# The g projections of layer 1 by seven block products, and the sums of weight blocks on GpSimd

## The chip, the core and the metric

The kernel runs on one core of a Trainium2 chip. The core has five engines with an instruction queue each: TensorE (PE, with its weight loads shown apart as PEld), VectorE (DVE), ScalarE (ACT), GpSimd (POOL) and SyncE (SP, which issues DMAs here). The metric is the device time of one execution in microseconds; lower is better.

## The reference

One step of a two-layer recurrent decoder for 512 prompt tokens and 8 sample tokens (520 columns, computed together). The change is in layer 1, the HGRN2 layer with 16 heads of 128:

```python
def layer_c(h, p, s_c, lb, norm_w, w_in, c_norm_w, w_out, ple_w, ple_g):
    u = rmsnorm(h, norm_w) @ w_in                       # 1024 -> 4 x 2048
    q, fx, v, gate = jnp.split(u, [HK_C, 2 * HK_C, 2 * HK_C + D_C], axis=-1)
    g = jnp.logaddexp(jnp.log(lb), jnp.log1p(-lb) + jax.nn.log_sigmoid(fx))
    k = (1.0 - lb) * jax.nn.sigmoid(-fx)
    o, new_c = hgrn2_scan(q * DK_C ** -0.5, k, v, g, s_c)   # per head, chunkwise
    o = o * lax.rsqrt(jnp.mean(o * o, axis=-1, keepdims=True) + EPS)
    o = o.reshape(Bsz, L, D_C) * c_norm_w * jax.nn.silu(gate)
    h = h + o @ w_out
    ...
```

In the kernel, f, v, q and g are the four projections fx, v, q and gate; g is only needed at the end of a head, as silu.

## The kernel before

All projections are done in halves of precision: each fp32 matrix is split into a rounded fp32r part and the rest, and a product is the sum of three matmuls, high by high, high by low, low by high. Activations are split once (`xh1`, `xl1`, each 8 slices of 128 rows by 520 columns). Weights are split as they come: a group of 256 columns (1 MB, tile `wraw`, two buffers) is loaded by SyncE, ScalarE writes the high part (`whir`, a CAST), VectorE the low part (`wlor`, wraw minus whir). In layer 1 these two are rings that hold four halves of 128x512.

Layer 1 goes through eight pairs of heads. A pair `pr` has four groups of weights in the order f, v, q, g; each yields 256 rows by 520 columns, that is 128 rows for each of its two heads. An ordinary projection (`project_both`) takes 8 slices x 3 x 2 column halves = 48 matmuls of 128x260 for each head. In pairs 1 to 7, f and v go another way, by `strassen`: the group is taken as a 2x2 block matrix (two halves of the 8 slices, two heads), the activations as 2x2 as well (two halves of the slices, two column halves), and seven block products of 4 x 3 = 12 matmuls stand in for eight. For that, sums of weight blocks are needed, four for each group, each 128x512, done in place or into the tiles named f1s, v1s and so on; sums of the activation blocks (`uh`, `ul`) are made once. The products come out in PSUM (tiles `sm` and `sg`) and are summed on VectorE into the SBUF tiles `l1a` (f) and `l1b` (v and g). Between the products TensorE does the heads' own work (A, kt, kv, o, ot, vt), and every second round the output projection (tile `o`), whose results are added to `h`.

q and g of every pair, and all of pair 0, are ordinary projections. `evac_g` takes a finished g tile from PSUM: ScalarE writes tanh(g/2) to `l1b`, VectorE makes (tanh + 1) times the PSUM tile.

GpSimd does little in layer 1: the small powers by which the heads normalize (`at__`, 128x4 and 16x1).

No order is written by hand. The code records operations, and `Plan.order` sets them out, engine by engine, from a cost for each operation, with engines as independent of one another; each engine then runs its list in order. Operations that TensorE's main products need are given urgency; some copies and scalings may go to ScalarE or VectorE, as the plan finds room. Nearly every instruction therefore has the line of the recording helper, L520, and tiles tell them apart. The change thus moves the order all through layer 1.

Of the kernel before, what the change touches and what calls it, by code (L numbers as in the profile page):

```python
# [15 lines left out]
AF = mybir.ActivationFunctionType  # L16
# [5 lines left out]
MUL, ADD, SUB, MAX, MIN = ALU.mult, ALU.add, ALU.subtract, ALU.max, ALU.min  # L22
# [3 lines left out]
N = T + NS  # L26
HN = N // 2
# [182 lines left out]
class Plan:  # L210
# [53 lines left out]
    @contextmanager  # L264
    def block(self, main=False):

        self.open = Op(self, self.pos + self.shift, 0)
        self.open.forms["pe"] = [[], 0.0, None]
        self.open.main = main
        self.open.ins, self.open.outs = [], []  # L270
        yield
        op, self.open = self.open, None
        op.forms["pe"][1] /= 2400.0
        self.add(op, op.ins, op.outs)
# [266 lines left out]
def hybrid_decode_step_kernel(ctx: ExitStack, tc: tile.TileContext, I, O, mode="both"):  # L541
# [19 lines left out]
    act, dve, pool, pe, sp = (Engine(plans, k) for k in ("act", "dve", "pool", "pe", "sp"))  # L561
    side, block = (lambda *a, **k: plans[-1].side(*a, **k)), (lambda *a: plans[-1].block(*a))

    def new(pool_, shape, tag, name, bufs=1, dt=F32):
        return plans[-1].tile(pool_, shape, dt, tag, name, bufs, {"psm": PSUM, "psa": PSUM, "drp": DRAM}.get(pool_, SBUF))
# [4 lines left out]
    def mmps(name):  # L570
        return new("psm", [128, 2, 512], "mm", name, 2)

    def grab(name):

        return new("psa", [128, 512], "ax", name)

    def halves(ap):
        return ap.rearrange("p (a b) -> p a b", a=2)

    def ps520(ps):  # L580
        return ps[:, :, :HN]
# [4 lines left out]
    def tt(out, a, b, op, eng=dve):  # L586
        eng.tensor_tensor(out=out, in0=a, in1=b, op=op)

    def stt(out, a, s, b, op0, op1):
        dve.scalar_tensor_tensor(out=out, in0=a, scalar=s, in1=b, op0=op0, op1=op1)  # L590
# [7 lines left out]
    def fn(out, in_, func, **kw):  # L598
        act.activation(out, in_, func, **kw)

    def copy(out, in_):

        plans[-1].record(("act", "copy", (out, in_), {}), ("dve", "tensor_copy", (out, in_), {}))
# [6 lines left out]
    def slot(tag, name, shape=None, dt=F32):  # L610
        return new("lay", shape or [128, KT, N], tag, name, dt=dt)
# [17 lines left out]
    def load_group(g):  # L629
        ap, k0, kk, c, w = groups[g]  # L630
        r = new("wp", [128, 2048], "raw", f"wraw{g}", 2)
        v = r[:, :kk * w].rearrange("p (k c) -> p k c", k=kk)
        with side(*((plans[-1].shift, 0.0, True) if plans[-1].pinned else (-LOAD_AHEAD,))):
            sp.dma_start(out=v, in_=ap[k0 * 128:(k0 + kk) * 128, c:c + w].rearrange("(k p) c -> p k c", p=128))
        raw_of[g] = v
# [9 lines left out]
    def split_half(v):  # L645

        hv, lv = (r.rearrange("p (k c) -> p k c", k=4) for r in ring_space(1))
        with side(-SPLIT_AHEAD):
            act.copy(hv, v)
            tt(lv, v, hv.bitcast(F32), SUB)  # L650
        return hv, lv
# [300 lines left out]
    mx, e0, e1, sm, lb, omlb, lb60, oml60, lbf, omf, cneg, cq, ch, fb = (lbt[:, i] for i in range(14))  # L952
# [658 lines left out]
    def layer1_fast():  # L1611
        NO = 4
        A = None
        B = slot("acy", "l1b", [128, 4160])
# [42 lines left out]
        H = [{} for _ in range(NH)]  # L1657

        def start_f(hd):
            nonlocal A  # L1660
            d, p = H[hd], hd % 2
            if A is None:
                A = slot("w", "l1a", [128, 4160])
            d["t"] = A[:, p * N:(p + 1) * N]
            d["b"] = A[:, 1040 + p * N:1040 + (p + 1) * N]

            d["s4"] = s4s[hd // 2 % 2][:, :, p]
            return d["t"]

        def done_f(hd, tanh=True):  # L1670
            d = H[hd]
            if tanh:
                fn(d["t"], d["t"], AF.Tanh, scale=0.5)
            t = d["t"][:, T:]
            ts(d["s4"][:, 0], t, -1.0, ADD, cneg[:, hd:hd + 1], MUL)
            ts(d["s4"][:, 1], t, ch[:, hd:hd + 1], MUL, fb[:, hd:hd + 1], ADD)
# [6 lines left out]
        def done_v(hd):  # L1683
            d, v = H[hd], B[:, hd % 2 * N:(hd % 2 + 1) * N]
            copy(d["s4"][:, 3], v[:, T:])
            with side(V_LATE):
# [3 lines left out]
                        pe.transpose(pv[:, c * 128:(c + 1) * 128], v[:, c * 128:(c + 1) * 128], ident)  # L1690
                copy(d["vt"], pv)

        def evac_f(hd):
            def f(ps):
                fn(halves(start_f(hd)), ps520(ps), AF.Tanh, scale=0.5)
                done_f(hd, False)
            return f
# [7 lines left out]
        def strassen(pr, names):  # L1705

            pss, n = [], 0

            def product(u, x):
                nonlocal n  # L1710

                i = n % 6
                if i % 3 == 2:
                    out = grab(f"sg{pr}_{n}")[:, :HN]
                else:
                    if i < 2:
                        pss[i:] = [mmps(f"sm{pr}_{n}")]
                    out = pss[i % 3][:, i // 3, :HN]
                n += 1
                hw, lw = u  # L1720
                for k in range(4):
                    with block(True):
                        for i, (w, b) in enumerate(((hw, x[0]), (hw, x[1]), (lw, x[0]))):
                            pe.matmul(out, lhsT=w[:, k], rhs=b[:, k], start=(k == 0 and i == 0), stop=(k == 3 and i == 2))
                    plans[-1].pos += 0.334
                return out

            def steps(nm):
                e, e1 = 2 * pr, 2 * pr + 1
                start, done = (start_f, done_f) if nm == "f" else (start_v, done_v)  # L1730
                o0, o1 = start(e), start(e1)
                l0, r0, l1, r1 = o0[:, :HN], o0[:, HN:], o1[:, :HN], o1[:, HN:]
                g = units[sec[f"{nm}{pr}"]][0]
                if g not in raw_of:
                    load_group(g)
                v = raw_of[g]
                a11, a12, a21, a22 = v[:, :4, :128], v[:, 4:, :128], v[:, :4, 128:], v[:, 4:, 128:]
                s2, s3 = (new("cst", [128, N], "sgt", f"{nm}{pr}s{i}", 2)[:, :512].rearrange("p (k c) -> p k c", k=4)
                          for i in range(2))
                w = split_half(a11)  # L1740
                with side(-SPLIT_AHEAD):
                    tt(s3, a11, a21, ADD)
                    tt(a21, a21, a22, ADD)
                    tt(s2, a21, a11, ADD)
                p1 = product(w, x11)
                copy(l0, p1)
                p6 = product(split_half(s2), u2)
                tt(r0, l0, p6, ADD)
                p7 = product(split_half(s3), t3)
                tt(l1, p7, r0, SUB)  # L1750
                w = split_half(a12)
                with side(-SPLIT_AHEAD):
                    tt(a12, a12, s2, ADD)
                p2 = product(w, x21)
                tt(l0, l0, p2, ADD)
                p5 = product(split_half(a21), u1)
                tt(r1, l1, p5, SUB)
                tt(r0, r0, p5, ADD)
                p3 = product(split_half(a12), x22)
                tt(r0, r0, p3, ADD)  # L1760
                done(e)
                p4 = product(split_half(a22), u4)
                tt(l1, l1, p4, ADD)
                done(e1)

            for nm in names:
                steps(nm)
# [9 lines left out]

        def evac_g(hd):
            def f(ps):
                sg = H[hd]["sg"] = B[:, 1040 + (hd % 2) * N:1040 + (hd % 2 + 1) * N]  # L1780
                fn(halves(sg), ps520(ps), AF.Tanh, scale=0.5)
                stt(halves(sg), halves(sg), 1.0, ps520(ps), ADD, MUL)
            return f
# [136 lines left out]
        def pair(pr, names):  # L1920
            a = 2 * pr
            if pr:
                strassen(pr, names[:2])
                with side(DECAY_LATE):
                    decay(a)
                names = names[2:]
            for nm in names:
                ev = {"f": evac_f, "v": evac_v, "q": evac_q, "g": evac_g}[nm]
                tiles = [(sec[f"{nm}{pr}"] + i, 0, ev(a + i), f"{nm}{a + i}") for i in range(2)]
                if pr == 0 and nm == "f":  # L1930
                    project_both(tiles, XN, K8)
                else:
                    for t in tiles:
                        project_both([t], XN, K8)
                if nm == "f":
                    with side(DECAY_LATE):
                        decay(a)
                if nm == "q" and pr in (2, 4, 6):
                    chunk(f"o{pr}", 2 * pr - 4, 2 if pr == 6 else 4, add_to_h)
# [325 lines left out]
```

## Time and profile before

| | |
|---|---|
| median of 3 runs | 1056.26 us (1055.57 to 1057.36) |
| profiled execution | 1052.58 us, span of its instructions 1050.9 us |
| granted TensorE clock | 0.994 |
| layer 1's heads in the trace | about 447 to 952 us |

Durations below come from the profiled execution, which is 3.7 us shorter than the median. On the page, busy is time in which an engine works; matmuls are pipelined, so their durations overlap. In names, `l1a<-l1a,sm` is the tile written and those read.

### The profile page before, as it was taken

What the parts mean: (1) busy time and instruction counts of PE and PEld (TensorE: products, weight loads), DVE (VectorE), ACT (ScalarE), POOL (GpSimd) and SP (SyncE); (2) the same over time, 40 slices, a digit from 0 to 9 for tenths busy, and PEclk for the clock granted to TensorE, in tenths of its full rate; (3) what the DMA queues carried; (4) which work ended last, traced back from release to release, by engine and by line L of the source; (5) the groups of instructions that cost most, each with busy time, mean ns of one, the idle gap of its engine ahead of it and who ended that gap; (6) DMA issues with size and microseconds to landing.
All of it is one profiled execution on the core that took longest, in us unless ns stands there. A gap on an engine that the chain in (4) does not pass through costs nothing.

```text
span 1050.9 us, 21517 instructions
## 1 busy us (share of the span) xinstructions
PE 1023.1 (97%) x8427; PEld 1000.0 (95%) x8427; DVE 832.6 (79%) x1705; ACT 630.8 (60%) x1482; POOL 139.4 (13%) x241
## 2 busy tenths in 40 slices
PE   9989899999999999999999999999999999999995
PEld 8989899899999999999999999999999999999995
DVE  6789788998996656697989759698598979868853
ACT  6588876654673222365676726678268685764553
POOL 4635854100000000001000000001000000100000
PEclk9999999999999999999999999999999999999998
DMA  9712254336586223553353433433434443553311
GB/s 285 246 30 92 81 166 141 122 110 191 188 257 213 89 98 117 153 203 90 98 149 109 142 91 108 139 100 113 122 90 139 124 116 111 137 180 121 121 41 45
DMA packets 129957, 138.45 MB, mean 132 GB/s; under 512 B 13704, under 2 KB 111128, under 8 KB 129832
## 3 DMA queue, kind: packets, MB, share of 16 engines
q1 hardware_dynamic: 129464, 136.64, 42.6%
q8 instruction: 68, 1.11, 0.4%
q10 hardware_dynamic: 160, 0.30, 0.1%
q14 instruction: 41, 0.34, 0.1%
q0 software_dynamic: 224, 0.06, 0.0%
HBM read 111.71 MB, written 25.44 MB: 131 GB/s over the span
## 4 chain that ended last, share of the span: by engine, by line
PE 73%; DVE 10%; DMA 6%; ACT 4%; POOL 3%; issue 2%; SPq 0%; POOLq 0%; ACTq 0%; DVEq 0%
PE o L520 10%; PE sm L520 9%; PE q L520 9%; PE pg L520 9%; PE g L520 8%; PE ob L520 4%; PE sg L520 4%; PE xbc L520 2%; PE ax L520 2%; DVE wlo L520 2%; PE oa L520 2%; PE pl L520 2%; PE z L520 1%; DMA smp<-in_state_b_ssm_dram 1%; POOL csm L520 1%
## 5 line engine op out<-in xcount | busy, mean ns | idle before, releaser
L520 ACT CAST whir<-wraw 128x512 fp32r<-128x512 f32 (+1 forms) x121 | 96.3, 798 | 83.9 <-PE o L520 40.6
L520 DVE TENSOR_TENSOR wlor<-wraw,whir 128x512 fp32r<-128x512 f32 (+1 forms) x121 | 109.6, 910 | 12.5 <-ACT whir L520 12.1
L520 ACT CAST whi<-wraw 128x1024 fp32r<-128x1024 f32 (+1 forms) x56 | 57.8, 1032 | 48.6 <-PE ob L520 34.5
L520 POOL TENSOR_TENSOR at__1738<-at__1738,nhalf 128x4 f32<-128x4 f32 (+1 forms) x24 | 22.6, 942 | 461.5 <-DVE at__1738 L520 455.5
L520 DVE TENSOR_TENSOR wlo<-wraw,whi 128x1024 fp32r<-128x1024 f32 (+1 forms) x64 | 77.3, 1208 | 8.0 <-ACT whi L520 7.4
L520 PE MATMUL o<-ohl,whir 128*128 128x260 f32 x512 | 83.0, 284 | 0.0
L520 PEld LDWEIGHTS o<-ohl,whir 128*128 128x128 f32 x512 | 70.0, 188 | 0.9 <-issue 0.6
L520 PE MATMUL g<-xh,whir 128*128 128x260 f32 x256 | 54.6, 294 | 1.1 <-DVE l1a L520 1.1
L520 PE MATMUL q<-xh,whir 128*128 128x260 f32 x256 | 53.2, 289 | 0.0
L520 PE MATMUL q<-xh,wlor 128*128 128x260 f32 x256 | 51.5, 283 | 0.0
L520 PE MATMUL q<-xl,whir 128*128 128x260 f32 x256 | 51.4, 282 | 0.0
L520 PE MATMUL g<-xl,whir 128*128 128x260 f32 x256 | 51.4, 282 | 0.0
L520 PE MATMUL g<-xh,wlor 128*128 128x260 f32 x256 | 51.4, 282 | 0.0
L520 PE MATMUL o<-ohl,wlor 128*128 128x260 f32 x256 | 51.4, 282 | 0.0
L520 DVE TENSOR_TENSOR h<-h,o 128x520 f32<-128x520 f32 x40 | 27.8, 694 | 26.2 <-PE o L520 25.9
L515 ACT ACT_TABLE_LOAD x36 | 46.2, 1283 | 0.6
L520 PE MATMUL sm<-uh,whir 128*128 128x260 f32 x140 | 40.4, 289 | 1.8 <-DVE l1a L520 1.6
L520 PE MATMUL sm<-xh,whir 128*128 128x260 f32 x140 | 41.4, 296 | 0.0
L520 PEld LDWEIGHTS g<-xh,whir 128*128 128x128 f32 x256 | 39.2, 189 | 2.2 <-DVE l1a L520 1.3
L520 PE MATMUL sm<-xh,wlor 128*128 128x260 f32 x140 | 39.6, 283 | 0.3 <-DVE wlor L520 0.3
L520 PE MATMUL xbc<-xnh,whi 128*128 128x260 f32 x192 | 39.7, 289 | 0.0
L520 PE MATMUL sm<-xl,whir 128*128 128x260 f32 x140 | 39.6, 283 | 0.0
(609 smaller groups left out, 3594.2 us busy)
## 6 DMA issues: line engine op xcount, KB each, us to landing
wraw<-in_c_w_in_dram SPq DMA_DIRECT2D x32, 1024.0 KB
wraw<-in_ab_w_in_dram SPq DMA_DIRECT2D x15, 1024.0 KB
wraw<-in_ab_w_out_dram SPq DMA_DIRECT2D x8, 1024.0 KB
wraw<-in_ple_gate_dram SPq DMA_DIRECT2D x8, 1024.0 KB
wraw<-in_c_w_out_dram SPq DMA_DIRECT2D x8, 1024.0 KB
pl<-pl_d SPq DMA_DIRECT2D x2, 2080.0 KB
smp<-in_state_b_ssm_dram SPq DMA_DIRECT2D x8, 512.0 KB
acy<-acsT_d SPq DMA_DIRECT2D x8, 512.0 KB
```

The source lines that it names most:

```text
L515: self.engines["act"].preload_act_table_set(SETS[table])
L520: getattr(f, name)(*a, **k)
```

## The change

The groups g of pairs 1 to 7 go through `strassen` too, each in a call of its own, with `start_g` and `done_g` at its ends. `done_g` takes the tanh from SBUF into the pair's f buffer `t` and multiplies in SBUF. The sums of weight blocks of all three (f, v and g) are recorded for GpSimd instead of VectorE.

```diff
+        def start_g(hd):
+            sg = H[hd]["sg"] = B[:, 1040 + (hd % 2) * N:1040 + (hd % 2 + 1) * N]
+            return sg
+
+        def done_g(hd):
+            sg, t = H[hd]["sg"], H[hd]["t"]
+            fn(t, sg, AF.Tanh, scale=0.5)
+            stt(sg, t, 1.0, sg, ADD, MUL)
...
                 with side(-SPLIT_AHEAD):
-                    tt(s3, a11, a21, ADD)
-                    tt(a21, a21, a22, ADD)
-                    tt(s2, a21, a11, ADD)
+                    tt(s3, a11, a21, ADD, pool)
+                    tt(a21, a21, a22, ADD, pool)
+                    tt(s2, a21, a11, ADD, pool)
...
                 with side(-SPLIT_AHEAD):
-                    tt(a12, a12, s2, ADD)
+                    tt(a12, a12, s2, ADD, pool)
...
             for nm in names:
+                if pr and nm == "g":
+                    strassen(pr, nm)
+                    continue
```

GpSimd's list, from the end of layer 1's set-up: before, only the heads' powers stand there.

```order
L520 AFFINE_SELECT l1d<-l1d 128x128
L520 AFFINE_SELECT l1d<-l1d 128x32 x2
L520 TENSOR_TENSOR at__1738<-at__1738,nhalf 128x4
L520 TENSOR_TENSOR at__1738<-at__1738,nhalf 16x1
L520 TENSOR_TENSOR at__1738<-at__1738,nhalf 128x4
```

Now, at g of pair 1 and at f and v of pair 2 (g1s, f2s, v2s are the sums' own tiles, wraw_6376 is g's group, wraw_6517 and wraw_6778 are those of f and v):

```order
L520 TENSOR_TENSOR g1s_6454<-wraw_6376 128x512
L520 TENSOR_TENSOR wraw_6376<-wraw_6376 128x4x128
L520 TENSOR_TENSOR g1s_6593<-wraw_6376 128x512
L520 TENSOR_TENSOR f2s_6614<-wraw_6517 128x512
L520 TENSOR_TENSOR wraw_6376<-wraw_6376,g1s_6593 128x4x128
L520 TENSOR_TENSOR wraw_6517<-wraw_6517 128x4x128
L520 TENSOR_TENSOR f2s_6824<-wraw_6517 128x512
L520 TENSOR_TENSOR v2s_6857<-wraw_6778 128x512
L520 TENSOR_TENSOR wraw_6517<-wraw_6517,f2s_6824 128x4x128
L520 TENSOR_TENSOR wraw_6778<-wraw_6778 128x4x128
L520 TENSOR_TENSOR v2s_6962<-wraw_6778 128x512
L520 TENSOR_TENSOR wraw_6778<-wraw_6778,v2s_6962 128x4x128
```

Twelve sums of 128x512 have come into its list here, one behind the other, with the powers behind them.

VectorE's list during g of pair 1, before (l1d and at__ belong to the heads, wraw_6513 is f's group of pair 2, g_6604 the g tile in PSUM):

```order
L520 TENSOR_TENSOR wlor_5463<-wraw_6513,whir_5439 128x512
L520 SCALAR_TENSOR_TENSOR l1a<-l1a 128x512
L520 TENSOR_TENSOR wraw_6513<-wraw_6513 128x4x128
L520 TENSOR_SCALAR at__1738<-at__1738,lbt 128x1
L520 TENSOR_TENSOR f2s_6699<-wraw_6513 128x512
L520 TENSOR_SCALAR l1d<-kv_6686,at__1738 128x128
L520 SCALAR_TENSOR_TENSOR l1d<-l1d,at__1738 128x128 x2
L520 SCALAR_TENSOR_TENSOR l1b<-l1b,g_6604 128x520
```

And now (smg and sgg are g's products in PSUM; sqt and l1d the sample states):

```order
L520 TENSOR_TENSOR l1b<-sgg_2_6734,l1b 128x260
L520 SCALAR_TENSOR_TENSOR sqt<-l1d,sqt 128x128
L520 TENSOR_TENSOR wlor_5611<-wraw_6376,whir_5532 128x512
L520 TENSOR_TENSOR l1b<-l1b,smg_0_6640 128x260
L520 SCALAR_TENSOR_TENSOR l1d<-sqt,l1d 128x128
L520 TENSOR_TENSOR wlor_5611<-wraw_6517,whir_5532 128x512
L520 TENSOR_TENSOR l1b<-l1b,smg_1_6669 128x260 x2
L520 SCALAR_TENSOR_TENSOR sqt<-l1d,sqt 128x128 x2
```

The sums for f have gone, and in their place stand half splits of g's blocks and sums of its products.

More of the change, by code (lines that the diff above doesn't have):

```diff
@@ L1713, in product @@
                 if i % 3 == 2:
-                    out = grab(f"sg{pr}_{n}")[:, :HN]
+                    out = grab(f"sg{names}{pr}_{n}")[:, :HN]
                 else:
                     if i < 2:
-                        pss[i:] = [mmps(f"sm{pr}_{n}")]
+                        pss[i:] = [mmps(f"sm{names}{pr}_{n}")]
                     out = pss[i % 3][:, i // 3, :HN]
@@ L1729, in steps @@
                 e, e1 = 2 * pr, 2 * pr + 1
-                start, done = (start_f, done_f) if nm == "f" else (start_v, done_v)
+                start, done = {"f": (start_f, done_f), "v": (start_v, done_v), "g": (start_g, done_g)}[nm]
                 o0, o1 = start(e), start(e1)
@@ L1779, in f @@
             def f(ps):
-                sg = H[hd]["sg"] = B[:, 1040 + (hd % 2) * N:1040 + (hd % 2 + 1) * N]
+                sg = start_g(hd)
                 fn(halves(sg), ps520(ps), AF.Tanh, scale=0.5)
```

## Prediction

> **What bounds the kernel now.** I read the page's busy times first, then busy times by stretch, then TensorE's waits, then groups of instructions inside layer 1 and last the places where GpSimd works beside VectorE.
>
> ```profile
> PE 1023.1 (97%) x8427; PEld 1000.0 (95%) x8427; DVE 832.6 (79%) x1705; ACT 630.8 (60%) x1482; POOL 139.4 (13%) x241
> ...
> DVE  6789788998996656697989759698598979868853
> ...
> POOL 4635854100000000001000000001000000100000
> ```
>
> GpSimd is free in the second half, where the change is. The next view gives, for a stretch in us: its length, then busy PE, PEld, DVE, ACT and POOL (instructions behind each), clock, DMA. The first row is all of layer 1's heads. The next three are round 1: the f and v products, then q, then g. The last four are rounds 1 to 7 without the three stretches of output-projection work that stand between.
>
> ```profile
> 447.00:952.00 505.00, 501.42 (x4162) 492.64 (x4162) 416.61 (x953) 338.58 (x840) 27.34 (x33) 1.00 0.42 123
> ...
> 504.70:530.40 25.70, 25.18 (x206) 24.11 (x205) 23.97 (x60) 15.77 (x44) 2.63 (x3) 1.00 0.52 142
> 530.40:542.80 12.40, 12.40 (x107) 12.39 (x106) 10.09 (x19) 11.00 (x22) 0.00 (x0) 1.00 0.41 129
> 542.80:560.90 18.10, 18.10 (x155) 17.75 (x154) 16.19 (x46) 14.97 (x46) 0.00 (x0) 1.00 0.31 81
> ...
> 504.70:597.10 92.40, 91.78 (x760) 89.63 (x758) 81.62 (x195) 66.81 (x168) 5.15 (x6) 1.00 0.45 129
> 621.20:731.30 110.10, 108.08 (x894) 105.58 (x893) 92.39 (x222) 79.74 (x202) 5.71 (x6) 1.00 0.42 122
> 754.30:863.40 109.10, 108.48 (x902) 106.33 (x901) 95.02 (x228) 77.42 (x198) 5.14 (x6) 1.00 0.43 123
> 878.20:949.30 71.10, 70.84 (x595) 69.77 (x594) 56.31 (x143) 48.76 (x132) 6.02 (x5) 1.00 0.47 141
> ```
>
> TensorE is the bound: 501.4 of 505.0 us busy, at full clock. But VectorE is close behind: in the f and v stretch 23.97 of 25.70 us (93%), in the g stretch 16.19 of 18.10. Over the last four rows it is busy 81.62 + 92.39 + 95.02 + 56.31 = 325.3 of 382.7 us. The waits of TensorE in layer 1 (total, times, longest) are still small, and all are for VectorE:
>
> ```profile
> PE sm L520 <- DVE l1a L520: 1.6, 3, 0.5
> PE g L520 <- DVE l1a L520: 1.1, 1, 1.1
> PE o L520 <- DVE l1d L520: 0.4, 2, 0.2
> PE sm L520 <- DVE wlor L520: 0.3, 1, 0.3
> ```
>
> **The change on TensorE.** A pair's g took 2 tiles x 8 slices x 3 x 2 halves = 96 matmuls, and takes 7 products x 4 x 3 = 84. Seven pairs lose 84. The chain of waits (start, length, what) gives the pace of one product:
>
> ```profile
> 521.46 1.44 PE sg L520 x12
> ```
>
> so 0.120 us each, all of it on the path: 84 x 0.120 = 10.1 us gone, if nothing else ends up last.
>
> **VectorE's and ScalarE's own work.** Groups inside 447 to 952 us (count, busy us, mean ns of one):
>
> ```profile
> L520 DVE TENSOR_TENSOR wlor<-wraw,whir 128x1024 fp32r<-128x1024 f32 x47 | 57.4, 1221 | 5.4 <-ACT whir L520 5.4
> L520 DVE TENSOR_TENSOR wlor<-wraw,whir 128x512 fp32r<-128x512 f32 x70 | 47.3, 684 | 6.8 <-ACT whir L520 6.7
> ...
> L520 DVE SCALAR_TENSOR_TENSOR l1b<-l1b,g 128x520 f32<-128x520 f32 x16 | 11.1, 694 | 2.0 <-ACT l1b L520 1.6
> ...
> L520 DVE TENSOR_TENSOR wraw<-wraw 128x512 f32<-128x512 f32 x14 | 9.6, 683 | 0.0
> L520 DVE TENSOR_TENSOR l1b<-l1b,sm 128x260 f32<-128x260 f32 x21 | 8.8, 421 | 1.3 <-PE sm L520 0.5
> ...
> L520 DVE COPY l1a<-sm 128x260 f32<-128x260 f32 x4 | 1.7, 420 | 0.1
> ```
>
> ```profile
> L520 ACT CAST whir<-wraw 128x1024 fp32r<-128x1024 f32 x47 | 49.1, 1045 | 49.1 <-PE o L520 27.0 <-issue 8.8 <-PE q L520 7.2
> L520 ACT CAST whir<-wraw 128x512 fp32r<-128x512 f32 x70 | 43.0, 618 | 21.2 <-PE sg L520 11.7 <-PE sm L520 5.0 <-DVE wraw L520 2.3
> ```
>
> Out of a pair's g on VectorE go two splits at 1.221 and two gate products at 0.694; in come seven half splits at 0.684, seven sums of products at 0.421, one copy at 0.420 (counted in full though ScalarE may take it) and again two gate products: 4.79 + 2.95 + 0.42 - 2.44 = +5.7 us, 40.0 in seven pairs. The 56 sums of weight blocks of f and v that leave it are 56 x 0.683 = 38.2. Net +1.7 us: VectorE's own load stays. ScalarE gets 7 x 0.618 - 2 x 1.045 = +2.2 a pair, +16 us in all on 338.6 of 505: no bound. A g tile's last gate product comes one sum (0.42 us) and the tanh later; its reader is the head's last product, a round's tail, so I cost that at nothing. That tanh is written to the pair's f buffer, which the next pair's first f product overwrites 1.44 us later at the earliest: nothing either. The DMA issues stay the same in number; g's raw buffer is let go only at its last split. The load that follows into it is v's of the next pair, and the whole f stage (12 matmuls x 7 = 10.1 us) covers it; without that cover the v sums come late, which is a rival below. The two banks that g's products now borrow from the heads' four I cost at nothing too; the covers are the other two.
>
> **The sums on GpSimd.** There are now 12 a pair, 84 in all, each of 128x512 with two inputs. No row has that; the nearest, the same operation at 32 and at 80 columns, are
>
> ```profile
> L520 POOL TENSOR_TENSOR lbt<-lbt 128x32 f32<-128x32 f32 x5 | 1.2, 239 | 1.3 <-ACT lbt L520 1.1
> L520 POOL TENSOR_TENSOR dtt<-dtt,hb 128x80 f32<-128x80 f32 x1 | 0.4, 358 | 0.0
> ```
>
> (358 - 239) / 48 = 2.48 ns a column, so 0.358 + 432 x 0.00248 = 1.43 us, twice VectorE's 0.683. From below it is bounded by the only long row, GpSimd's select of 128x1024 with one input, 1.09 us (next fence). 84 x 1.43 = 120 us of GpSimd in 505: GpSimd itself is no bound. What matters is what VectorE does meanwhile. The first answer is of one operation's duration, least, median and greatest; the second is in order of time.
>
> ```profile
> L520 POOL TENSOR_SCALAR_AFFINE_SELECT wsl<-acy x8: 1088/1092/1890, 147.4 to 225.4; 128x1024 f32<-128x1024 f32 x8
> ...
> L520 DVE TENSOR_TENSOR wsl<-wsl,at__1738 x8: 674/683/1480, 173.0 to 233.6; 128x512 f32<-128x512 f32 x8
> ```
>
> ```profile
> 205.35 1.09 POOL L520 TENSOR_SCALAR_AFFINE_SELECT wsl<-acy 128x1024 f32<-128x1024 f32 x1 [7.30 <-PE yd L520]
> ```
>
> ```profile
> 147.83 2.56 DVE L520 TENSOR_SCALAR smp<-smp,sfm 128x128 f32<-128x128 f32 x4
> ...
> 194.25 1.56 DVE L520 TENSOR_TENSOR wlo<-wraw,whi 128x1024 fp32r<-128x1024 f32 x1
> ...
> 205.51 1.48 DVE L520 TENSOR_TENSOR wsl<-wsl,at__1738 128x512 f32<-128x512 f32 x1
> ```
>
> ```profile
> L520 DVE SCALAR_TENSOR_TENSOR xa<-sga,xa x8: 691/698/1583, 226.2 to 275.3; 128x520 f32<-128x520 f32 x8
> ...
> L520 DVE SCALAR_TENSOR_TENSOR bcs<-bcs,pt x12: 734/744/1356, 101.0 to 180.2; 128x512 f32<-128x512 f32 x12
> ...
> L520 DVE TENSOR_SCALAR smp<-smp,sfm x28: 273/280/1126, 147.0 to 292.7; 128x128 f32<-128x128 f32 x28
> ...
> L520 DVE SCALAR_TENSOR_TENSOR bcs<-csm x4: 151/152/1070, 142.7 to 185.9; 128x8 f32<-128x8 f32 x4
> ```
>
> At 205.35 the select begins, at 205.51 a VectorE product that takes 0.683 us elsewhere begins and takes 1.480: it ends when GpSimd is done. Each greatest value in these rows lies at one of the eight selects. The losses are 0.846 twice (the four at 147.83), 0.797, 0.885, 0.612, 0.918 and some 0.33 (the 1.56 against 1.22), and one select met nothing: 5.23 us over eight selects, 0.65 each, 60% of the select's 1.09. In turn two selects needed 1.9 us. The instructions hit have two inputs in SBUF (or are plain SBUF scalings); in layer 1 the splits, the sample scans and the gate products are of that kind, while the sums that read a product from PSUM are not.
>
> The Trainium skill, "SBUF — State Buffer", section "Who interferes with whom", states the same as a rule: a VectorE instruction with two SBUF inputs and a GpSimd one that reads SBUF cannot run together, and the second waits for the whole of the first. By that rule a sum could cost VectorE up to its whole length; the rows above agree. "GPSIMD Engine Reference", section "Elementwise — side-by-side cycle accounting", gives 4497 ns for an addition of 2048 columns; a quarter, 1.12 us, would make the loss 0.67 and the sum below 5.5 us faster instead of slower, so by that page it is a close call.
>
> I take the loss in proportion: 0.65 x 1.43 / 1.09 = 0.85 us a sum, since the same operation's rows are nearer than the select's; the ends are nothing (all in VectorE's idle time) and the whole 1.43.
>
> **The sum.** Nine sums (g of pairs 2, 4 and 6, three each) can run in the output stretches, where VectorE has room. 75 x 0.85 = 64 us. VectorE then needs 325.3 + 1.7 + 64 = 391.0 us in the stretches that TensorE would do in 382.7 - 10.1 = 372.6. The later one ends: 391.0 - 382.7 = +8.3 us. VectorE keeps some unavoidable idle time (more) and some instructions' tails overlap when they stand close (less); I let these cancel. The profiled execution took 1052.6 us, 3.7 under the median of the runs; on the median it is 1056.3 + 8.3 = about 1064.
>
> **Rivals.** (1) Faster: the sums fall mostly into VectorE's idle time, of which the four rows have 57.4 us. Below a loss of (372.6 - 327.0) / 75 = 0.61 us a sum TensorE stays the bound and the full 10.1 us come off: 1046. For it: the select's own 0.65 is nearly there, and half the sums run in q and early g stretches, where VectorE idles 10 to 20%; against: in the v stage it hardly idles. (2) No difference: losses of 0.71 to 0.77 a sum, around the break-even (382.7 - 327.0) / 75 = 0.74. (3) Slower by more: the sums come too late for the products, since three follow each other on GpSimd (up to 3 x 1.9) and queue with the heads' powers. Before, they run far ahead:
>
> ```profile
> L520 DVE TENSOR_TENSOR f2s<-wraw x2: 681/682/683, 540.9 to 549.8; 128x512 f32<-128x512 f32 x2
> ```
>
> is 20 us before the f products at 560.9, so it decides only if weights land less than some 7 us ahead; at 1 us for each of 21 stages, TensorE otherwise the bound, it gives 1056.3 - 10.1 + 21 = 1067. The powers behind the sums would delay ScalarE's normalization, not TensorE at once.
>
> **How the numbers follow.** A difference under 0.2% (2.1 us) can't be told from none. The forecast, VectorE as the bound through GpSimd, has 0.50 (1059 to 1082; 1082 is a loss of 1.08 us a sum: 75 x 1.08 = 81, +25), rival 3 has 0.06, rival 1 has 0.33, rival 2 0.11. Slower is 0.56, faster 0.33, same 0.11. The range goes from rival 1's 1046 to 1082.
>
> **What would show it.** In the profile after: 84 sums on GpSimd of 1.4 us or more; half splits on VectorE clearly over 0.684 us in the mean; VectorE's busy time in layer 1 up from 416.6 by some 60 us; new waits of TensorE for wlor and for evacuations, far over the 0.3 and 1.6 us above. Half splits still at 0.69, or VectorE stretched while TensorE never waits, would make it wrong and the time fall toward 1046.

## The result and the profile after

| | before | after |
|---|---|---|
| median | 1056.81 us (1055.57 to 1058.14, 4 runs) | 1090.22 us (1088.9 to 1093.44, 4 runs) |
| ratio | | 1.0317 [1.0292, 1.0343] |
| profiled execution | 1052.58 us, span 1050.9 | 1093.44 us, span 1091.6 |
| rounds 1 to 7 in the trace | 504.7 to 949.3, 444.6 us | 512.0 to 986.9, 474.9 us |

The change costs 33 us, against 8 forecast. The page's rows of busy time, GpSimd's slices and the granted clock by slice, after:

```profile
PE 1027.9 (94%) x8343; PEld 998.5 (91%) x8343; DVE 887.3 (81%) x1753; ACT 635.8 (58%) x1496; POOL 267.7 (25%) x325
...
POOL 4635845100000000013233122331233322320000
PEclk9999999999999999999999999999999998999997
```

The 84 matmuls are gone (8427 to 8343). Below are sums over all stretches of one kind between the first f product of round 1 and the last g product of round 7: length, then busy PE, PEld, DVE, ACT, POOL. In order: the f and v products, q, g, the output projection, and the whole (there the clock follows). Before:

```profile
sum 170.70, PE 168.68 PEld 162.79 DVE 158.35 ACT 105.37 POOL 16.55; mean PE 24.10 PEld 23.26 DVE 22.62 ACT 15.05 POOL 2.36
...
sum 94.30, PE 94.30 PEld 94.29 DVE 69.62 ACT 81.33 POOL 3.31; mean PE 13.47 PEld 13.47 DVE 9.95 ACT 11.62 POOL 0.47
...
sum 117.70, PE 116.19 PEld 114.23 DVE 97.36 ACT 86.03 POOL 2.17; mean PE 16.60 PEld 16.32 DVE 13.91 ACT 12.29 POOL 0.31
...
sum 61.90, PE 61.90 PEld 61.55 DVE 38.97 ACT 25.85 POOL 0.00; mean PE 20.63 PEld 20.52 DVE 12.99 ACT 8.62 POOL 0.00
...
504.70:949.30 444.60, 441.07 (x3659) 432.86 (x3658) 364.30 (x858) 298.57 (x755) 22.02 (x23) 1.00 0.42 122
```

And after:

```profile
sum 195.70, PE 174.62 PEld 165.51 DVE 181.75 ACT 111.22 POOL 62.56; mean PE 24.95 PEld 23.64 DVE 25.96 ACT 15.89 POOL 8.94
...
sum 98.00, PE 94.45 PEld 93.25 DVE 78.19 ACT 74.26 POOL 30.55; mean PE 13.49 PEld 13.32 DVE 11.17 ACT 10.61 POOL 4.36
...
sum 111.90, PE 107.08 PEld 104.81 DVE 98.06 ACT 73.21 POOL 34.66; mean PE 15.30 PEld 14.97 DVE 14.01 ACT 10.46 POOL 4.95
...
sum 69.30, PE 67.32 PEld 65.92 DVE 59.61 ACT 42.70 POOL 12.99; mean PE 22.44 PEld 21.97 DVE 19.87 ACT 14.23 POOL 4.33
...
512.00:986.90 474.90, 443.47 (x3562) 429.48 (x3560) 417.62 (x907) 301.39 (x763) 140.76 (x103) 0.98 0.39 110
```

The f and v stretches grow by 25.0 us and g's shrink by 5.8. VectorE is busy for 53.3 us more, yet still idle for 57 of 474.9 us; TensorE, idle for 3.5 us before, is idle for 31.4. Its waits in layer 1 are now (total, times, longest):

```profile
PE smfv L520 <- DVE l1a L520: 8.0, 5, 3.2
PE os L520 <- DVE l1d L520: 7.9, 6, 2.9
PE q L520 <- DVE wlor L520: 3.6, 3, 2.1
PE smfv L520 <- DVE wlor L520: 3.0, 2, 2.3
```

One such wait, at its place in the timeline (start, us, engine). GpSimd:

```profile
515.04 1.88 POOL L520 TENSOR_TENSOR wraw<-wraw,f1s 128x512 f32<-128x512 f32 x1 [3.01 <-DVE wlor L520]
516.88 1.35 POOL L520 TENSOR_TENSOR wraw<-wraw 128x512 f32<-128x512 f32 x1
518.31 1.31 POOL L520 TENSOR_TENSOR v1s<-wraw 128x512 f32<-128x512 f32 x1
```

VectorE, and behind it TensorE:

```profile
515.68 1.38 DVE L520 SCALAR_TENSOR_TENSOR l1c<-l1d,l1c 128x128 f32<-128x128 f32 x1
516.99 0.41 DVE L520 TENSOR_TENSOR l1a<-l1a,smfv 128x260 f32<-128x260 f32 x1
517.33 1.05 DVE L520 SCALAR_TENSOR_TENSOR l1d<-l1c,l1d 128x128 f32<-128x128 f32 x1
518.30 1.74 DVE L520 SCALAR_TENSOR_TENSOR l1c<-l1d,l1c 128x128 f32<-128x128 f32 x2
...
521.76 0.41 DVE L520 TENSOR_TENSOR l1a<-l1a,smfv 128x260 f32<-128x260 f32 x1
```

```profile
522.32 0.36 PE L520 MATMUL smfv<-uh,whir 128*128 128x260 f32 x1 [1.93 <-DVE l1a L520]
```

Four sample scans of 0.34 us take 4.2 us beside three sums; the sum from PSUM between them (0.41) is not held. The product at 522.32 waits 1.93 us for a PSUM bank that a late sum of products (521.76) has to empty. Then, by microseconds (busy PE, PEld, DVE, ACT, POOL, clock):

```profile
523.00:524.00 1.00, 1.00 (x9) 1.00 (x8) 1.00 (x5) 0.00 (x0) 0.00 (x0) 0.73 0.84 189
524.00:525.00 1.00, 1.00 (x7) 1.00 (x7) 1.00 (x5) 0.00 (x0) 0.00 (x0) 0.50 0.98 180
525.00:526.00 1.00, 1.00 (x6) 1.00 (x6) 0.44 (x3) 0.55 (x1) 0.82 (x1) 0.50 1.03 247
526.00:527.00 1.00, 1.00 (x7) 1.00 (x6) 0.82 (x3) 0.32 (x2) 0.21 (x1) 0.56 1.08 383
```

the clock falls to a half for 3.4 us: another 1.7 us gone (0.27 + 0.50 + 0.50 + 0.44). In rounds 1 to 7, 8.5 us go this way; before, none.

### The profile page after: what moved, and what is told of

Same layout as the page of the kernel before. It is cut to its first block, busy times and chain, and to the rows that moved or that the text cites. A ratio compares the mean times of both kernels' runs of the same rounds, so it can differ in the third digit from the quotient of the medians.

```text
span 1091.6 us, 21591 instructions
## 1 busy us (share of the span) xinstructions
PE 1027.9 (94%) x8343; PEld 998.5 (91%) x8343; DVE 887.3 (81%) x1753; ACT 635.8 (58%) x1496; POOL 267.7 (25%) x325
## 5 line engine op out<-in xcount | busy, mean ns | idle before, releaser
L520 PE MATMUL smfv<-uh,whir 128*128 128x260 f32 x140 | 41.2, 295 | 9.7 <-DVE l1a L520 8.0
L520 PE MATMUL smfv<-xh,whir 128*128 128x260 f32 x140 | 41.0, 293 | 3.2 <-ACT whir L520 1.7
L520 PE MATMUL smfv<-uh,wlor 128*128 128x260 f32 x140 | 40.9, 292 | 3.1 <-DVE wlor L520 3.0
L520 PEld LDWEIGHTS q<-xh,wlor 128*128 128x128 f32 x256 | 39.4, 188 | 4.3 <-DVE wlor L520 4.2
L520 PEld LDWEIGHTS o<-ohl,wlor 128*128 128x128 f32 x256 | 39.4, 188 | 1.1 <-DVE wlor L520 1.1
L520 PE MATMUL smfv<-xh,wlor 128*128 128x260 f32 x140 | 40.0, 286 | 0.2
L520 PE MATMUL smfv<-ul,whir 128*128 128x260 f32 x140 | 40.0, 286 | 0.0
L520 PE MATMUL smfv<-xl,whir 128*128 128x260 f32 x140 | 39.8, 284 | 0.0
L520 PEld LDWEIGHTS q<-xl,whir 128*128 128x128 f32 x256 | 39.4, 188 | 0.0
L520 PEld LDWEIGHTS q<-xh,whir 128*128 128x128 f32 x256 | 39.3, 189 | 0.1
## 6 DMA issues: line engine op xcount, KB each, us to landing
smp<-in_state_b_ssm_dram SPq DMA_DIRECT2D x8, 512.0 KB
acy<-acsT_d SPq DMA_DIRECT2D x8, 512.0 KB
```

Source lines behind the costliest of these rows:

```text
L520: getattr(f, name)(*a, **k)
```

## The experiments

My theory: GpSimd's reads hold VectorE, and each hold-up costs its time where VectorE is dense, whatever idle time it has elsewhere. Rivals: the new order of g costs the time by itself; the sums come late; any work of GpSimd does it. "Rounds" is the length of rounds 1 to 7 in each trace (444.6 before), "DVE" VectorE's busy time there, "half clock" what 1 minus the granted clock sums to.

| run | ratio | rounds | DVE | half clock |
|---|---|---|---|---|
| after | 1.0317 [1.0292, 1.0343] | 474.9 | 417.6 | 8.5 |
| e1_sums_dve | 1.0269 [1.0231, 1.0307] | 460.9 | 402.5 | 5.1 |
| e2_fv_gpsimd | 1.0102 [1.0076, 1.0129] | 453.5 | 364.9 | 1.7 |
| e3_write_only | 0.9974 [0.9954, 0.9995] | 438.0 | 362.8 | 0.0 |
| e12_write_wait | 1.0017 [0.9996, 1.0039] | 444.6 | 362.5 | 1.7 |
| e4_plan_knows | 1.0552 [1.0514, 1.0590] | 500.2 | 408.1 | 17.1 |
| e11_in_turn | 1.0353 [1.0298, 1.0408] | 473.3 | 418.6 | 8.5 |
| g246p | 1.0112 [1.0090, 1.0133] | 453.2 | 386.5 | 5.1 |
| e5_twins_fv | 1.0243 [1.0224, 1.0263] | 470.6 | 380.8 | 6.8 |
| e6_twins_q | 1.0082 [1.0061, 1.0104] | 448.2 | 381.1 | 1.7 |
| e7_memsets_fv | 1.0318 [1.0295, 1.0341] | 477.7 | 364.7 | 11.9 |
| e8_half_fv | 1.0063 [1.0042, 1.0085] | 451.9 | 372.9 | 1.7 |
| e9_half_memsets | 1.0011 [0.9994, 1.0029] | 446.3 | 364.0 | 0.0 |
| e10_half_q | 1.0028 [1.0010, 1.0047] | 446.7 | 373.5 | 0.0 |

**The two parts alone.** e1_sums_dve keeps g's seven products and does all sums on VectorE:

```diff
-tt(s3, a11, a21, ADD, pool)
+tt(s3, a11, a21, ADD)          # and the other three
```

> The new kernel with all 84 sums of weight blocks recorded for VectorE again (g still by seven products). Theory (GpSimd's reads hold VectorE up): GpSimd is out of it, but VectorE's own work grows by 40 us for g and 28 x 0.683 = 19 us for its sums, to some 476 us of 495 in layer 1; 1058 to 1075. Rival A (the sums come late because GpSimd is slow and works in order): sums are quick again, under 1052. Rival B (g by seven products overloads VectorE, ScalarE or PSUM by itself): 1085 or more, as the new kernel.

1081.85 us, over my theory's 1075 and near the 1085 of rival B. Much of the loss is there without GpSimd: 26.0 us of 33.4 by the medians, 16.3 of 30.3 in the rounds of the two traces. VectorE's 402.5 us and TensorE's 431 (441.1 less 10.1) would both fit into 434.5 (444.6 less 10.1); the rounds took 460.9, with TensorE waiting for VectorE in new places:

```profile
PE o L520 <- DVE l1a L520: 5.1, 3, 2.1
PE o L520 <- DVE h L520: 3.0, 3, 1.9
```

TensorE's idle time lies in all stretches here (f and v 6.9 us, q 7.9, g 4.2, output 3.9), though VectorE is busy for only 77% of q's (83.3 of 108.0). Load and order changed together, so what decides there stays open.

e2_fv_gpsimd leaves g an ordinary projection and has GpSimd do the sums of f and v:

```diff
-if pr and nm == "g":
+if False and nm == "g":
```

> The new kernel with g as ordinary projections again: only the 56 sums of f and v on GpSimd. Theory: VectorE loses 38 us of work and gets back 56 x 0.63 = 35 us of hold-ups, no gain on TensorE; 1054 to 1064. Rival A: lateness remains for 14 of 21 stages, 1070 to 1080. Rival B: 1050 to 1056, VectorE having more room than before.

1065.76 us, a little over the theory's 1064. VectorE's total does not move (364.3 to 364.9): what the sums gave back, the hold-ups took. But they took it in other places. f and v, and the whole:

```profile
sum 181.80, PE 173.14 PEld 166.08 DVE 173.60 ACT 129.12 POOL 65.15; mean PE 24.73 PEld 23.73 DVE 24.80 ACT 18.45 POOL 9.31
...
509.40:962.90 453.50, 443.50 (x3647) 433.75 (x3647) 364.91 (x818) 293.04 (x734) 97.59 (x75) 1.00 0.40 119
```

The f and v stretches have 15.3 us more of VectorE and are 11.1 longer; 4.5 of these are TensorE's own work that the plan put there. The other stretches together have 14.6 us less of VectorE and are 2.2 shorter, about what TensorE has less to do in them (2.0). The same total, spread otherwise, comes with 9 us more of rounds; 1.7 us of half clock is in it, and late sums may have a part.

**Reads or not.** e3_write_only has the lists of after, but each sum of weight blocks is three memsets of its output.

```diff
+if op.taken == "pool" and calls[0][0] == "tensor_tensor" and _free(calls[0][2]["out"]) == 512:
+    calls = [("memset", (calls[0][2]["out"], 0.25), {})] * 3
```

> The new kernel, planned alike (same lists on the other engines), but each sum on GpSimd is replaced by three memsets of its output, so GpSimd is as long at work and later work waits for it as before, and reads nothing from SBUF; the sums themselves are left out. Theory (GpSimd's reads against VectorE's second input): half splits on VectorE back to 0.69 us, VectorE's busy time in layer 1 down by some 50 us, 1044 to 1054. Rival A: late sums remain, 1080 to 1092. Rival B: 1080 to 1092.

1052.32 us. Such a memset of a sum's own tile no longer waits for the weights to land, so this took two things away. e12_write_wait gives the second back: the first of the three memsets writes the loaded block.

```diff
+first = k["in1"] if <the first sum of a group> else k["out"]
+calls = [("memset", (x, 0.25), {}) for x in (first, k["out"], k["out"])]
```

> The write-only kernel (memsets in place of the sums of weight blocks, which are left out) with the waits for the loads kept: of the three memsets that stand for the first sum of a group, the first now writes the loaded weights themselves, so that GpSimd waits for the load there as it does in the changed kernel. Theory (reads are the main loss): 1052 to 1060 us. Rival (the queue's wait for the loads is the main loss): 1070 us or more.

1057.64 us, as the theory had it. GpSimd is busy as long as after (142.2 against 140.8 us), in the same order and again waiting for the loads, and VectorE's half splits are back at 685 ns; the rounds and two of TensorE's waits stand below:

```profile
L524 DVE TENSOR_TENSOR wlor<-wraw,whir 128x512 fp32r<-128x512 f32 x105 | 71.4, 685 | 13.5 <-ACT whir L524 12.6 <-POOL at__1738 L524 0.4
...
505.90:950.50 444.60, 434.15 (x3562) 423.37 (x3561) 362.53 (x903) 300.96 (x764) 142.16 (x262) 1.00 0.41 117
```

```profile
PE q L524 <- DVE wlor L524: 2.7, 3, 1.3
PE smfv L524 <- DVE l1a L524: 2.4, 2, 1.7
```

After, the same group reads

```profile
L520 DVE TENSOR_TENSOR wlor<-wraw,whir 128x512 fp32r<-128x512 f32 x105 | 86.0, 824 | 8.0 <-ACT whir L520 7.6
```

So GpSimd's reads, with all that follows from them, cost 1090.2 - 1057.6 = 32.6 us (31.7 by the ratios, as the two were run in different sessions): the whole loss. One difference is left: in e12 the sums are missing, so that the products get other values. e8 against e9 below, where no value differs, points the same way. Nor does e1 contradict this: there VectorE does the sums itself and is busy for 402.5 us of the rounds, 40 more than in e12, where no engine does them. The Trainium skill, "SBUF — State Buffer", section "Who interferes with whom", says that a VectorE instruction with two SBUF inputs contends with a GpSimd one that reads, not with one that only writes; 685 against 824 ns agrees. The other finding is that even without any hold-up the 10.1 us of matmuls are not gained. The waits for loads cost some 5 us of them (1052.3 to 1057.6, again from two sessions); where the rest stays is open.

**Place.** The next kernels are before with additions on GpSimd that nobody needs (the mask plus itself, 128x512, into scratch); the other engines keep their lists. e5_twins_fv has six behind each first-head power, e6_twins_q behind each second-head power, e7_memsets_fv has three memsets for each addition of the former.

```diff
+if <a power of the first head has been issued on GpSimd>:
+    for _ in range(6):
+        f.tensor_tensor(out=scr, in0=src, in1=src, op=ADD)
```

> The kernel before, with work added: behind each first-head pow of a round of layer 1 GpSimd does six additions of 128x512 (mask plus mask) into a scratch tile that nothing reads, 48 in all, in the stretches of the f and v products, where VectorE was busy for 158.4 of 170.7 us. The lists of the other four engines stay as before. Theory (a hold-up costs its full length where VectorE is dense): 48 x 0.65 to 0.75 = 31 to 36 us of VectorE's time, of which the 12 us of its idle time there take a part at most: +18 to +34 us, about 1075 to 1090 us. Rival (VectorE's idle time anywhere in a round cancels it, as the prediction's sum had it: 364.2 us busy of 444.5): +0 to +5 us, and the same as with the additions in the q stretches.

> The same 48 additions on GpSimd, behind each second-head pow, which lies in the stretches of the q products, where VectorE was busy for 69.7 of 94.4 us. The lists of the other four engines stay as before. Theory (place decides): the same 31 to 36 us of hold-ups, of which 25 us of idle time take most: +3 to +15 us, about 1059 to 1071 us, less than half of what they cost in the f and v stretches. Rival (only the number of additions counts): as much as there.

> As with the additions in the f and v stretches, but each addition is three memsets of the same 128x512 tile, about 1.6 us together: GpSimd is busy for as long, or longer, and writes as much, but reads nothing. Theory (VectorE is held by GpSimd's reads): within 2 us of the kernel before, and VectorE's busy time up by less than 5 us. Rival (GpSimd's late hand-over of its own next results, or any work of GpSimd, costs the time): +15 us or more.

The first two came out near the theory (1082.03 and 1065.47 us), but the control did not: 1090.5 us without any hold-up (VectorE 364.7 us). The reason is in TensorE's waits, additions first, then memsets:

```profile
PE ot6s L520 <- ACT l1d L520: 3.9, 1, 3.9
PE ot0s L520 <- ACT l1d L520: 3.0, 1, 3.0
```

```profile
PE ot6s L520 <- ACT l1d L520: 7.1, 1, 7.1
PE ot0s L520 <- ACT l1d L520: 5.4, 1, 5.4
```

The second head's power stood behind some 7.4 us of additions (9.5 of memsets), and ScalarE's normalization and a transposition behind it. My design made GpSimd late where it was needed; e5 and e7 show that price and cannot show the other. Four such waits, of 2.4 to 3.9 us behind 7.4 us of work, mean a slack of about 4 us, so I halved the load: three additions or seven memsets.

> The additions behind the first-head pow again, three at each pow, 24 in all, so that GpSimd's own next result, the second head's pow, is late by some 4 us and not 7.4 to 9.5; the four waits for it were 2.4 to 3.9 us long behind 7.4 us, and 4.8 to 7.1 behind 9.5, so that behind 4 us none should be left. The lists of the other engines stay as before. Theory (a hold-up costs its full length where VectorE is dense): 24 x 0.35 (the 16.5 us of busy time that 48 additions added) to 0.7 = 8 to 17 us of VectorE's time in the stretches of f and v, of which half or more reaches the end: +5 to +15 us, and more than twice what the same 24 cost in the q stretches. Rival (what the 48 cost there was GpSimd's lateness alone): +0 to +3 us.

> The control of the kernel with 24 additions in the f and v stretches: at each first-head pow seven memsets of the same tile, 3.7 us together, instead of three additions. GpSimd is late by as much and reads nothing. Theory: no wait is left at this lateness, and nothing holds VectorE: within 2 us of before. Rival (lateness costs from the first microsecond): as much as the additions.

> The same 24 additions, three at each second-head pow, in the stretches of the q products. Theory (place decides): 8 to 17 us of hold-ups fall into 25 us of VectorE's idle time: +0 to +4 us. Rival (place does not count): as much as in the f and v stretches.

Now the control stands at +0.1%, and place can be seen. The f and v stretches with 24 additions in them, the same stretches with the control's memsets, and q's with the 24 additions, in that order:

```profile
sum 176.40, PE 169.91 PEld 162.63 DVE 164.62 ACT 104.16 POOL 42.39; mean PE 24.27 PEld 23.23 DVE 23.52 ACT 14.88 POOL 6.06
```

```profile
sum 172.20, PE 169.11 PEld 162.62 DVE 157.27 ACT 104.67 POOL 42.20; mean PE 24.16 PEld 23.23 DVE 22.47 ACT 14.95 POOL 6.03
```

```profile
sum 95.30, PE 94.78 PEld 94.56 DVE 75.86 ACT 81.13 POOL 24.47; mean PE 13.54 PEld 13.51 DVE 10.84 ACT 11.59 POOL 3.50
```

With the additions VectorE is busy for 6.2 to 6.3 us more than before in either place. In the dense stretches that comes with 5.7 us of length, in q's with 1.0. Against the control it is 4.2 us of length for 7.4 us of VectorE in the dense stretches; q's have no such control. Over the rounds it is +7.3 (1.7 of it half clock) against +2.1. Place counts: the medians, of one session, are 1063.8 and 1059.1 us. That it counts more than twice, as the theory asked, is not settled: the ratios are +0.63% [0.42, 0.85] and +0.28% [0.10, 0.47].

**Other ways out.** e4_plan_knows tells the planner of the hold-ups, by 0.65 us more on VectorE's clock for each sum:

```diff
+if e == "pool" and calls[0][0] == "tensor_tensor" and _free(calls[0][2]["out"]) == 512:
+    clk["dve"] = max(clk["dve"], t) + 0.65
```

> The new kernel, but the planner is told that each 128x512 sum on GpSimd takes 0.65 us of VectorE's time. Same work, another order. Theory: VectorE's load stays, but side work is moved to where there is room; 1070 to 1085. Rival A: no change, 1086 to 1094. Rival B: no change.

A clear miss: 1114.58 us. The plan spread work otherwise (VectorE 9.5 us less busy), and TensorE's idle time rose to 50 us; I suppose that it cannot know which instruction will be hit, but no run shows that. e11_in_turn was for the late sums. After has, in round 3, f's last sum behind v's first, which waits for v's weights:

```profile
658.27 1.29 POOL L520 TENSOR_TENSOR v3s<-wraw 128x512 f32<-128x512 f32 x1 [5.25 <-DMA wraw<-in_c_w_in_dram]
659.52 1.29 POOL L520 TENSOR_TENSOR wraw<-wraw,f3s 128x512 f32<-128x512 f32 x1
```

```diff
+plans[-1].gate = last_sum     # the last sum of the group before
 tt(s3, a11, a21, ADD, pool)
+plans[-1].gate = None
```

> The changed kernel with GpSimd's list put in turn: the first sum of a group of weights is planned only behind the last sum of the group before it, so that f's last sum no longer stands behind a sum that waits for v's weights. Nothing else changes but a few rows. In the trace after, that wait put off f's last sum by some 2.4 us in rounds 3 and 5 (5.25 and 5.47 us of GpSimd waiting for the load), and a stretch of halved clock followed in both. Theory (hold-ups are the main loss, late sums a part): 5 to 12 us less than the changed kernel, about 1078 to 1085 us. Rival (late sums are the main loss): 1065 us or less. Rival (the late sums are only covered by other waits): 1090 us as before.

1092.57 us: the wait for v's weights fell to 0.9 and 1.3 us and nothing was gained. The stretch at half clock in round 3 is gone, but others came in rounds 2 and 4, again 8.5 us in all; my 5 to 12 us were wrong. g246p takes g's seven products in three pairs only, with 12 sums on GpSimd:

```diff
-if pr and nm == "g":
+if pr in (2, 4, 6) and nm == "g":
```

> A smaller change: the g projections go by seven products in pairs 2, 4 and 6 only, with only g's sums (12) on GpSimd; the sums of f and v stay on VectorE. TensorE has 36 products of 0.120 us = 4.3 us less, VectorE 3 x 5.7 = 17 us more, and 12 x 0.7 = 8 us of hold-ups. Theory: VectorE's dense stretches of f and v pay for what falls in them; if half of the 25 us does, +3 to +12 us less 4.3: 1055 to 1065 us. Rival (VectorE's idle time of a round, 80 us, takes it all): 1052 us, faster by 0.4%.

1066.44 us, a little over the theory's 1065, with room left on VectorE (386.5 of 453.2). Nothing here beats before by more than e3's 0.26%, and there the sums were not computed; so no better version is offered.

## Why the prediction was wrong

The mechanism that I named is there: VectorE is held by GpSimd's reads, and the signs that I had asked for came (half splits at 824 ns, VectorE 53 us busier, waits of up to 3.2 us). How this reaches the time is what I had wrong.

- **TensorE's gain**: 84 matmuls at 0.120 us left the list. Right as a count, but not collected: e12, with nothing held up, is at +0.17%. Its TensorE is busy for 6.9 us less than before in the rounds and idle for 6.9 more (444.60 less 434.15 is 10.4, against 3.5). The term was worth about nothing, not -10.1.
- **VectorE's own work**, +1.7 (40.0 less 38.2 is 1.8): right, and nearly nothing (e12: 362.5 against 364.3).
- **A sum's length**, 1.43 us: near. The 84 sums in the trace after take 1.52 us in the mean; one group of them, least, median and greatest ns:

```profile
L520 POOL TENSOR_TENSOR wraw<-wraw x21: 1259/1624/2220, 492.9 to 956.4; 128x512 f32<-128x512 f32 x21
```

- **The loss for a sum**, 0.85: too high. VectorE's busy time differs by 417.6 - 362.5 = 55.1 us between after and e12, over 80 sums in the rounds: 0.69. The select's own 0.65 was nearer than its scaling.
- **The sum** is the step that failed. I added VectorE's work of whole stretches of rounds, set it against TensorE's, and let the later one end. With the measured loss this would have been worse still: 325.3 + 1.7 + 75 x 0.69 = 378.8, 3.9 us under 382.7, gives 1052, a faster kernel; over whole rounds 362.5 + 55.1 = 417.6 us of VectorE against 434.5 of TensorE (444.6 less 10.1) gives rival 1's 1046. So that I forecast a slower kernel at all was luck, the work of a loss that was too high. In truth both engines waited in turn. In the f and v stretches VectorE was 93% busy before (158.35 of 170.70) and is 93% busy after (181.75 of 195.70); no run here got beyond 95.5% there (173.60 of 181.80 in e2). The 23.4 us of VectorE that came into them went with 25.0 us of length, 19.1 of it idle time of TensorE, while VectorE's 57 us of idle time, mostly elsewhere, stayed unused. I had written that idle time and overlapping tails cancel; the placement kernels show that they do not.
- **What the sum had no term for**: the clock. Half clock after TensorE's waits adds 8.5 us in the rounds after and 1.7 in e12.
- In all: I had the reads at 64 us of VectorE, of which 18.4 reach the end (8.3 over the 10.1); measured, 55 us and 32.6. That is 14.2 us of the miss, and the uncollected matmuls 11.8 (+1.7 instead of -10.1); together 26, the distance from 1064 to 1090.
- **Rivals**: 1 and 2 had the same fault. Rival 3, late sums, is visible in round 3, but e11 shows that mending it gains nothing beside the hold-ups, and e12, whose GpSimd waits for loads too, is at +0.17%.

In e12 to after, TensorE's idle time rises by 21.0 us and half clock by 6.8, 27.8 of 30.3 us of rounds; the rest I could not place. Open too: rounds begin 0.2 to 9.5 us later in the profiled runs of the other kernels than before, though there the lists hardly differ; half clock at 11 to 15 us explains 1.7 of it in after.

## What to carry to other kernels

Don't add an engine's work over stages when its idle time lies in other stages: lists run in order, and what landed in stretches where the engine was 93% busy went into the time for the larger part, though the mean said 82%. A lower share is no safeguard either, as q's stretches in e1 show: look at which wait ends last. GpSimd was a free helper here only for work that reads no SBUF while VectorE runs two-input work, and that nothing urgent in its own list has to wait for (e7). A wait of the bounding engine can cost more than its length: here one of 1.9 us cost 3.6.

## What the runs showed of the hardware

- TensorE's clock halved for about 3.4 us behind single waits of 1.15 us (e6, e8), 1.93 us and 3.19 us (after). The Trainium skill, "TensorE: Matmul & The Clock Gate", section "HAM oscillation — how this bites in real kernels", gives idle gaps over some 3.4 us as what to avoid; the halved stretches here are as long as its window, but shorter waits were enough. Not every one: the wait of 1.15 us, for `g` from `l1a`, passed at full clock before, in e9 and in e10, and two of 2.15 us passed in after.
- A hold-up did not scale with the held instruction: a scan of 0.34 us took 1.38 beside a sum, a half split of 0.685 us 0.824 in the mean.
- A GpSimd addition of a 128x512 tile to itself took 1.04 us in the median (e8, below), one of two blocks at least 1.26 (after):

```profile
L526 POOL TENSOR_TENSOR l1d<-l1d x24: 1030/1042/2315, 527.4 to 952.5; 128x512 f32<-128x512 f32 x24
```
